# A hybrid FoX/GLA decoder layer: gate folded into W_o, residual rows summed half-way, and FFN operands made in the order of their products

## The chip, the core and the metric

One core of one Trainium2 chip. The metric is the device time of one execution in microseconds (us), given as the median of several runs. Engines: TensorE (PE; its weight loads PEld), VectorE (DVE), ScalarE (ACT), GpSimd (POOL), and SyncE (SP), which issues the transfers.

## What is computed

One decoder layer of 1024 rows and width 1024, in float32. The parts that matter here, from the reference:

```python
u = x * (1.0 + scale_m) + shift_m
proj = u @ w_in                                  # FoX and GLA columns
...
y = jnp.concatenate([fox_out, gla_out], axis=-1) @ w_o
x = layer_norm(DEEPNORM_ALPHA * x + (1.0 + gate_m) * y, ln1_g, ln1_b)
u2 = x * (1.0 + scale_f) + shift_f
h = jax.nn.silu(u2 @ w_gate) * (u2 @ w_up)       # 1024 -> 2816
y2 = h @ w_down
x = layer_norm(DEEPNORM_ALPHA * x + (1.0 + gate_f) * y2, ln2_g, ln2_b)
```

## The kernel before

**Arithmetic.** Every float32 operand of a large product is split into a high part (a rounding cast by ACT, L87) and a low part (a subtraction by VectorE, L88). A product is three matmuls: high by high, high by low, low by high. `split` and `load_split` do this; a W_o load passes through a "raw" buffer (a ring of three, shared with other loads) and is split into buffers "hi" and "lo".

**Order.** A scheduler with a timeline simulation sets the order of the instructions on each engine; within an engine they run in that order. `tc.issue_after` (and `after(key)`) keeps what it encloses behind a named instruction.

**Stages.** Input projection and GLA come first (to about 366 us of the span). The FoX stage follows (366 to 572 us), in 16 steps of scores, softmax and values; into its first 12 steps 16 *fills* are put, `woproj_gla(h, t)`: 12 matmuls (L664 to L666) of the GLA half of y for a tile of 128 rows and 512 columns, an ACT copy to a raw buffer, and a store to the scratch tensor `yp_d`. The mixer's end runs in two halves of 512 rows, each of 8 *units* (`mixer_units`, 4 row tiles by 2 column halves h): 12 matmuls of the FoX half of y in a PSUM bank "yo" (L845 to L847), then VectorE adds the stored part (L848), POOL multiplies by the gate row `gm` (L849), VectorE forms alpha x + y (L850) and the LayerNorm statistics (L789); after h = 1 the row is scaled by ACT (L857) and stored. `mixer_loads` brings the rows of x and of `yp_d`, `mixer_weights` the FoX rows of W_o. The first half's units lie in the last FoX steps, the second half's behind them, up to 607 us.

**FFN.** Rows of u2 are transposed (u2p, L873) and scaled by ACT (L874), the first half of rows into tiles `af`, the second into `x2` (for the fourth chunk a raw buffer); a *chunk* j is 128 of the first 512 features together with 128 of the second 512. Gate and up products of one group f of 128 hidden columns (22 groups) are made by a Strassen-like form, with seven products of 12 matmuls (L965): p1 = B11 A11 and p2 = B21 A12 into "gu"; T3 S3 and T4 A22 into "gx"; T1 S1 and B22 S4 into "gy"; T2 S2 into "gz". A are quarters of u2 (A22 of the second rows), S1 to S4 their sums (S1 = A21 + A22, S3 = A11 - A21, S2 = S1 - A11, S4 = A12 - S2); B and T are quarters of the weights and their sums. `first_operands` makes A11 and A12; `second_operands` makes A22 and, chunk by chunk, S1 with S3 and then S2 with S4 (L910 to L919); `first_weights` splits the gate weights, `sum_weights` makes B22 and T1 to T4 (L947 on, sums L951 to L954). Five products (p1 of groups 0, 1, 2, p2 of 0 and 1) are queued behind the last unit, ahead of all products that use S. Later groups need no new S.

Of the kernel before, what the change touches and what calls it, by code (L numbers as in the profile page):

```python
# [33 lines left out]
def hymba_layer_kernel(  # L34
# [399 lines left out]
    wa2 = mp.tile([P, 256], F32R, tag="m1", name="wa2")[0:80]  # L434
# [73 lines left out]
    def gla_pair(p, n):  # L508
# [20 lines left out]
        osb = mp.tile([P, 256], F32, tag="m1", name=nm("osb"))  # L529
# [116 lines left out]
    yp_d = dp.tile([S, D], F32, name="yp_d")  # L646
    wo_g = {}

    def woproj_gla(h, t):
# [10 lines left out]
        ts = slice(t * P, (t + 1) * P)  # L660
        ps = bank("b3", "yg")
        for k in range(4):
            wh, wl = wo_g[h][k // 2]
            nc.tensor.matmul(ps, ogh[k][:, ts], wh[:, k % 2, :], start=k == 0, stop=False)  # L664
            nc.tensor.matmul(ps, ogh[k][:, ts], wl[:, k % 2, :], start=False, stop=False)
            nc.tensor.matmul(ps, ogl[k][:, ts], wh[:, k % 2, :], start=False, stop=k == 3)  # L666
# [137 lines left out]
    YS = ((4, 5, 6, 7), (10, 11, 12, 13))  # L804

    def mixer_loads(half):
        rt, yt = [], []
        for q in range(4):
            t = 4 * half + q
            r = slot(XS[half][q], name="r")  # L810
            nc.sync.dma_start(r, xr[t * P : (t + 1) * P, :])
            rt.append(r)
            y = slot(YS[half][q], name="yp")
            nc.sync.dma_start(y, yp_d[t * P : (t + 1) * P, :])
            yt.append(y)
        return rt, yt

    def mixer_weights(h):
        return [
            load_split(  # L820
                (2, 512),
                w_o[g * 256 : (g + 1) * 256, h * 512 : (h + 1) * 512].rearrange("(k p) n -> p k n", p=P),
            )
            for g in range(2)
        ]
# [4 lines left out]
    def mixer_units(half, rt, yt):  # L830
# [36 lines left out]
    S_HL = ((0, 1, 2, 3, 10), (11, 12, 13, 26, 27), (28, 29, 30, 31, 36), (20, 21, 22, 23, 37))  # L867
# [24 lines left out]
    def second_operands(rt):  # L892
# [7 lines left out]
        ops = {n: [] for n in ("A22", "S1", "S2", "S3", "S4")}  # L900
# [4 lines left out]
        for j in range(NJ):  # L905

            t = slot(S_HL[j][4], (2, 512), dt=F32R, name="a22")
            split(t[:, 0, :], t[:, 1, :], xs[j][:, 1, :])
            ops["A22"].append((t[:, 0, :], t[:, 1, :]))
            nc.vector.tensor_tensor(xs[j][:, 1, :], xs[j][:, 0, :], xs[j][:, 1, :], op=ALU.add)  # L910
            nc.vector.tensor_tensor(xs[j][:, 0, :], af[j][:, 0, :], xs[j][:, 0, :], op=ALU.subtract)
            hi = slot(S_HL[j][0], (2, 512), dt=F32R, name="s31h")
            lo = slot(S_HL[j][1], (2, 512), dt=F32R, name="s31l")
            split(hi, lo, xs[j])
            ops["S3"].append((hi[:, 0, :], lo[:, 0, :]))
            ops["S1"].append((hi[:, 1, :], lo[:, 1, :]))
        for j in range(NJ):
            nc.vector.tensor_tensor(af[j][:, 0, :], xs[j][:, 1, :], af[j][:, 0, :], op=ALU.subtract)
            nc.vector.tensor_tensor(af[j][:, 1, :], af[j][:, 1, :], af[j][:, 0, :], op=ALU.subtract)  # L919
            hi = slot(S_HL[j][2], (2, 512), dt=F32R, name="s24h")  # L920
            lo = slot(S_HL[j][3], (2, 512), dt=F32R, name="s24l")
            split(hi, lo, af[j])
            ops["S2"].append((hi[:, 0, :], lo[:, 0, :]))
            ops["S4"].append((hi[:, 1, :], lo[:, 1, :]))
        opnd.update(ops)
# [46 lines left out]
    def group_parts(f, w):  # L972
# [157 lines left out]
    for idx, (hp, i) in enumerate(steps):  # L1130
# [9 lines left out]
        if idx < len(nfill):  # L1140
            for _ in range(nfill[idx]):
                with (tc.issue_after(lastsc[(2, 2)].ins) if idx == 11 else nullcontext()):
                    woproj_gla(*fills.pop(0))
        if hp == 3 and i == 0:
            gm = wtile("raw", (D,), F32)
            nc.sync.dma_start(gm, grow_d[0, :].partition_broadcast(P))
            xa, ya = mixer_loads(0)
            late = mixer_units(0, xa, ya)
# [5 lines left out]
    xb, yb = mixer_loads(1)  # L1154
# [4 lines left out]
    for f in mixer_units(1, xb, yb):  # L1159
        f(3)  # L1160
    first_weights(load_gate(2), ws[2])
    second_operands(xb)
    gs = [group_parts(f, ws[f]) for f in range(3)]
    with after("yo"):
# [4 lines left out]
        gs[2][0]()  # L1169
    for f in range(NF):  # L1170
        if f < 3:
            p1, p2, p754, p63 = gs[f]
            w = ws[f]
            g = load_gate(f)
# [50 lines left out]
```

## Time and profile before

| | |
|---|---|
| median of the runs | 1318.05 us (1318.05, 1318.34, 1313.09) |
| the profiled execution | 1315.98 us, span 1314.2 us |
| busy, of the span | PE 96%, DVE 58%, ACT 38%, POOL 19% |
| mean granted TensorE clock | 0.989 of full |
| FoX stage, 366 to 572 us | PE 204.99 of 206 us busy |
| 560 to 660 us, in 20 us windows | PE 18.15, 17.57, 18.86, 6.57, 19.56 |

Times of the trace are us from the span's start. A row names the source line, the engine, the operation, out<-in by the program's names, and the shape; "xN" is a count. The median is over whole executions, and the trace is one of them.

### The profile page before, as it was taken

Reading aid. Unit: us, or ns where it says so; the run is one execution under the profiler, and the core shown is the slowest. Engines: PE = TensorE matmul, PEld = TensorE weight load, DVE = VectorE, ACT = ScalarE, POOL = GpSimd, SP = SyncE. Lnnn points to the kernel's source line nnn. Section 1 sums busy time; section 2 is a strip of 40 time slices with the busy share of each in tenths; the row PEclk is TensorE's granted clock in tenths of the full one; section 3 lists DMA queues with packets and bytes.
Section 4 is the critical chain, followed back from the end, with each engine's and each line's share of the span. In section 5 each row is a group of like instructions: output and inputs, shape, how many; then the busy total and the mean of one; then the engine's idle time right before and its main releaser. Section 6 shows DMA issues by size and latency. Waiting matters only on the chain.

```text
span 1314.2 us, 16370 instructions
## 1 busy us (share of the span) xinstructions
PE 1259.9 (96%) x6341; PEld 1018.3 (77%) x6341; DVE 756.2 (58%) x1093; ACT 497.1 (38%) x834; POOL 244.6 (19%) x244
## 2 busy tenths in 40 slices
PE   5999999999999999998599999999999999999997
PEld 4888987899876766667488888888888878788885
DVE  7665547732345546567965565565565576484346
ACT  3423355523265566464532233233323322411331
POOL 3500123320033435433000000000000076010004
PEclk9999999999999999999799999999999999999999
DMA  9875611102013206542342322321331474644431
GB/s 299 256 228 177 207 50 33 33 9 65 1 49 98 56 27 226 176 152 97 99 142 80 96 78 68 96 92 53 97 97 48 142 279 152 203 153 129 129 128 64
DMA packets 123534, 153.17 MB, mean 117 GB/s; under 512 B 6480, under 2 KB 86458, under 8 KB 123456
## 3 DMA queue, kind: packets, MB, share of 16 engines
q1 hardware_dynamic: 123456, 152.12, 36.1%
q8 instruction: 50, 0.82, 0.3%
q14 instruction: 28, 0.23, 0.1%
HBM read 123.64 MB, written 24.13 MB: 112 GB/s over the span
## 4 chain that ended last, share of the span: by engine, by line
PE 77%; DMA 8%; DVE 7%; ACT 3%; issue 2%; POOL 1%; SPq 1%; POOLq 0%; DVEq 0%; ACTq 0%
PE gx L965 9%; PE gy L965 9%; PE gu L965 9%; DMA wc<-in_w_c_dram 5%; PE dn L1059 5%; PE dn L1061 5%; PE dn L1060 5%; PE gz L965 5%; PE pv L756 4%; PE tr L746 3%; PE acc L330 2%; PE acc L331 2%; PE acc L332 2%; PE acc L100 2%; PE acc L101 2%
## 5 line engine op out<-in xcount | busy, mean ns | idle before, releaser
L88 DVE TENSOR_TENSOR lo<-raw,hi 128x1024 fp32r<-128x1024 f32 (+1 forms) x108 | 146.3, 1356 | 258.6 <-ACT hi L87 258.5
L87 ACT CAST hi<-raw 128x1024 fp32r<-128x1024 f32 (+1 forms) x108 | 113.1, 1049 | 192.3 <-PE dn L1061 79.3
L330 PE MATMUL acc<-hi,uh 128*128 128x264 f32 (+1 forms) x384 | 108.1, 282 | 1.0 <-ACT osb L530 0.8
L331 PE MATMUL acc<-lo,uh 128*128 128x264 f32 (+1 forms) x384 | 108.2, 282 | 0.0
L332 PE MATMUL acc<-hi,ul 128*128 128x264 f32 (+1 forms) x384 | 108.1, 282 | 0.0
L1032 POOL TENSOR_TENSOR r<-r,l1g 128x1024 f32<-128x1024 f32 x8 | 24.3, 3068 | 436.3 <-DMA r<-z_d 436.3
L1060 PE MATMUL dn<-lo,hh 128*128 128x512 f32 x256 | 101.2, 395 | 0.0
L1061 PE MATMUL dn<-hi,hl 128*128 128x512 f32 x256 | 100.8, 395 | 0.0
L1059 PE MATMUL dn<-hi,hh 128*128 128x512 f32 x256 | 94.2, 396 | 4.1 <-ACT hi L87 2.1
L721 DVE CUSTOM_DVE_ANT_0 pr<-sc,smask 128x128 f32<-128x128 f32 (+7 forms) x64 | 47.9, 755 | 55.2 <-PE sc L717 31.5
L330 PEld LDWEIGHTS acc<-hi,uh 128*128 128x128 f32 x384 | 72.2, 188 | 2.1 <-ACT osb L530 1.0
L331 PEld LDWEIGHTS acc<-lo,uh 128*128 128x128 f32 x384 | 72.2, 188 | 0.7 <-issue 0.5
L332 PEld LDWEIGHTS acc<-hi,ul 128*128 128x128 f32 x384 | 72.1, 188 | 0.3 <-issue 0.2
L965 PE MATMUL gu<-a1h,hi 128*128 128x512 f32 x160 | 63.6, 397 | 0.0
L965 PE MATMUL gu<-a1l,hi 128*128 128x512 f32 x160 | 63.5, 397 | 0.0
L965 PE MATMUL gu<-a1h,lo 128*128 128x512 f32 x160 | 63.3, 396 | 0.0
L731 POOL TENSOR_SCALAR pr<-pr,sm 128x128 f32<-128x128 f32 (+7 forms) x64 | 52.1, 816 | 57.3 <-DVE sm L728 56.8
L751 ACT COPY pt<-tr 128x512 f32<-128x512 f32 x80 | 46.1, 582 | 43.9 <-PE tr L746 42.3
L756 PE MATMUL pv<-pt,fv 128*64 128x256 f32 x320 | 61.4, 396 | 0.5 <-DVE ofl L88 0.5
L1059 PEld LDWEIGHTS dn<-hi,hh 128*128 128x128 f32 x256 | 48.2, 189 | 16.6 <-ACT hi L87 2.8
L100 PE MATMUL acc<-ul,hi 128*128 128x512 f32 x144 | 58.0, 403 | 0.0
L101 PE MATMUL acc<-uh,lo 128*128 128x512 f32 x144 | 57.9, 402 | 0.0
(305 smaller groups left out, 3103.0 us busy)
## 6 DMA issues: line engine op xcount, KB each, us to landing
raw<-in_w_down_dram SPq DMA_DIRECT2D x44, 512.0 KB, 3.9
wc<-in_w_c_dram SPq DMA_DIRECT2D x32, 512.0 KB, 4.4
raw<-in_w_gate_dram SPq DMA_DIRECT2D x25, 512.0 KB, 3.9
h_d<-hf SPq DMA_DIRECT2D x22, 512.0 KB, 2.7
hr<-h_d SPq DMA_DIRECT2D x22, 512.0 KB, 3.9
u<-in_w_up_dram SPq DMA_DIRECT2D x21, 512.0 KB, 3.8
wc<-in_w_c_dram SPq DMA_DIRECT2D x32, 256.0 KB, 6.7
raw<-in_w_in_dram SPq DMA_DIRECT2D x15, 512.0 KB, 4.0
```

The source lines that it names most:

```text
L87: nc.scalar.copy(dst_hi, src)
L88: nc.vector.tensor_tensor(dst_lo, src, dst_hi.bitcast(F32), op=ALU.subtract)
L100: nc.tensor.matmul(ps, lh, rl, start=False, stop=False)
L101: nc.tensor.matmul(ps, ll, rh, start=False, stop=stop)
L330: nc.tensor.matmul(ps, uh[k][:, ts], wh[:, k % 4, :], start=k == 0, stop=False)
L331: nc.tensor.matmul(ps, uh[k][:, ts], wl[:, k % 4, :], start=False, stop=False)
L332: nc.tensor.matmul(ps, ul[k][:, ts], wh[:, k % 4, :], start=False, stop=k == NK - 1)
L756: nc.tensor.matmul(pv[64 * par : 64 * par + 64, 0:256], fv_t(kb)[:, 64 * h : 64 * h + 64], pt[:, par, a * 256 : (a + 1) * 256], start=kb == 0,
L965: nc.tensor.matmul(ps, x, y, start=start and j == 0 and i == 0, stop=j == NJ - 1 and i == 2, skip_group_check=not start,)
L1059: nc.tensor.matmul(ps, hh, wh, start=i == 0 and a == 0, stop=False)
L1060: nc.tensor.matmul(ps, hh, wl, start=False, stop=False)
L1061: nc.tensor.matmul(ps, hl, wh, start=False, stop=i == NF // 2 - 1 and a == 1)
```

## The change

1. **Gate in W_o.** `wo_load` loads 256 rows by 512 columns of W_o, and POOL multiplies both blocks by `gm` (two 128x512 operations per load, 24 in all) ahead of the split. The units' 16 multiplies go. `gm` takes one raw buffer from the first FoX step to the last W_o load.
2. **Half-way rows.** A fill ends with one VectorE operation, alpha x + PSUM, on an x tile of 128x512 loaded for it (three tiles in turn), stored to `rp_d`; 16 x loads are added, the ACT copies go. `mixer_loads` reads four tiles of `rp_d` per half where it read four of x and four of `yp_d`. A unit is one add (PSUM + r), then the statistics.
3. **Operands in the order of the products.** `second_operands` is made in stages, all four chunks of one operand before the next: S3, S1, A22, S2, S4, each in 128x512 pieces.
4. **Group 0's weight sums** (`sum_weights(0)`) stand after the fifth of the second half's eight units; they stood behind `second_operands`.
5. **Six products** are queued ahead of the S products: p2 of group 2 is added; its p1 is copied to a tile of its own.
6. Storage: osb, wa2, B22 and one S3 tile take other slots.

```diff
     def split(dst_hi, dst_lo, src):
         nc.scalar.copy(dst_hi, src)
-        nc.vector.tensor_tensor(dst_lo, src, dst_hi.bitcast(F32), op=ALU.subtract)
+        return nc.vector.tensor_tensor(dst_lo, src, dst_hi.bitcast(F32), op=ALU.subtract).ins
...
+    def wo_load(r0, h, slots=None):
+        raw = wtile("raw", (2, 512), F32)
+        hs = slice(h * 512, (h + 1) * 512)
+        nc.sync.dma_start(raw, w_o[r0 : r0 + 256, hs].rearrange("(k p) n -> p k n", p=P))
+        for k in range(2):
+            nc.gpsimd.tensor_tensor(raw[:, k, :], raw[:, k, :], gm[:, hs], op=ALU.mult)
...
+        split(hi, lo, raw)
+        return hi, lo
...
+    def x_load(n):
+        if n < 2 * NT:
+            h, t = divmod(n, NT)
+            b = xbuf[:, n % 3, :] if n % 3 < 2 else xlast
+            nc.sync.dma_start(b, xr[t * P : (t + 1) * P, h * 512 : (h + 1) * 512])
+            xt.append(b)
...
-        yt = wtile("raw", (512,), F32)
-        nc.scalar.copy(yt, ps)
-        nc.sync.dma_start(yp_d[ts, h * 512 : (h + 1) * 512], yt)
+        with after("yg"):
+            x_store()
+        b = xt[n]
+        nc.vector.scalar_tensor_tensor(b, b, ALPHA, ps, op0=ALU.mult, op1=ALU.add)
+        yt.append((h, t, b))
+        with tc.issue_after(ins.ins):
+            x_load(n + 2)
...
-            nc.vector.tensor_tensor(yp[:, hs], ps, yp[:, hs], op=ALU.add)
-            nc.gpsimd.tensor_tensor(yp[:, hs], yp[:, hs], gm[:, hs], op=ALU.mult)
-            nc.vector.scalar_tensor_tensor(r[:, hs], r[:, hs], ALPHA, yp[:, hs], op0=ALU.mult, op1=ALU.add)
+            nc.vector.tensor_tensor(r[:, hs], r[:, hs], ps, op=ALU.add)
...
+        stage("S3", 0, a11, a11, a21, ALU.subtract, "t")
+        stage("S1", 1, a21, a21, a22, ALU.add, "sS3")
+        stage("A22", 4, a22, None, None, None, "sS1")
+        stage("S2", 2, a22, a22, a11, ALU.subtract, "lo")
+        stage("S4", 3, a12, a12, a22, ALU.subtract, "sS2")
...
-    for f in mixer_units(1, xb, yb):
+    late = mixer_units(1, xb)
+    for f in late[:5]:
+        f(3)
+    g = load_gate(0)
+    sum_weights(0, g, load_up(0), ws[0])
+    for f in late[5:]:
         f(3)
     first_weights(load_gate(2), ws[2])
-    second_operands(xb)
+    x2 = second_rows(xb)
+    second_operands(x2)
...
         gs[2][0]()
+        gs[2][1]()
```

A stage makes, for each chunk, one sum (VectorE) and its split (ACT cast, VectorE subtraction); its last argument names the instruction behind which it is issued ("t" the last split of group 0's T, "lo" the last split of A22, "sS3" the last S3 difference, and so on). Line numbers in the rows of the changed order are those of the changed file.

**Places in the order.** TensorE, at the end of the last product that needs no S (names: b1 and hi/lo of a gu row are gate weights of a group, a1 operands A11 and A12; hi_1005 and hi_921 hold T3 and T2 of group 0, hi_1007 and hi_923 T1 and T4). Before:

```order
L965 MATMUL gu_998_5740<-a1h_922_5397,b1_934_5427 128x512
L965 MATMUL gu_998_5740<-a1h_927_5414,b1_933_5426 128x512
L965 MATMUL gu_998_5740<-a1l_928_5415,b1_933_5426 128x512
L965 MATMUL gu_998_5740<-a1h_927_5414,b1_934_5427 128x512
L965 MATMUL gx_1009_5825<-s31h_979_5685,hi_1005_5817 128x512
L965 MATMUL gx_1009_5825<-s31l_980_5686,hi_1005_5817 128x512
L965 MATMUL gz_1011_5865<-s24h_990_5718,hi_1005_5817 128x512
L965 MATMUL gz_1011_5865<-s24l_991_5719,hi_1005_5817 128x512
L965 MATMUL gy_1010_5839<-s31h_979_5685,hi_1007_5821 128x512
```

Now:

```order
L996 MATMUL gu_966_5738<-a1h_888_5385,b1_894_5397 128x512
L996 MATMUL gu_966_5738<-a1l_889_5386,b1_894_5397 128x512
L996 MATMUL gu_966_5738<-a1h_888_5385,b1_895_5398 128x512
L996 MATMUL gx_970_5818<-s3_946_5663,hi_921_5530 128x512 x2
L996 MATMUL gx_970_5818<-s3_946_5663,lo_922_5531 128x512
L996 MATMUL gx_970_5818<-s3_947_5667,hi_921_5530 128x512 x2
L996 MATMUL gx_970_5818<-s3_947_5667,lo_922_5531 128x512
L996 MATMUL gx_970_5818<-s3_948_5671,hi_921_5530 128x512
```

Before, gx, gz and gy took turns by single matmuls as chunk 0's operands came; now whole chunks of S3 follow one another, and the first gy stands behind two of them and a half. Ahead of the first gx stand now, from the first gu on, 36 gu matmuls, 16 transposes, 22 gu matmuls, 16 transposes and 14 gu matmuls; the first matmul with the low part of group 1's T3 and T2 is the 135th that is no transpose.

VectorE behind the last LayerNorm row (af are the first rows, x2 and raw_937/raw_969 the second; L88 the low parts; L951 and L952 sums of group 0's weights). Before:

```order
L88 TENSOR_TENSOR a22_978_5680<-x2_966_5628,a22_978_5680 128x512
L910 TENSOR_TENSOR x2_966_5628<-x2_966_5628 128x512
L911 TENSOR_TENSOR x2_966_5628<-af_909_5350,x2_966_5628 128x512
L88 TENSOR_TENSOR a22_981_5689<-x2_967_5629,a22_981_5689 128x512
L918 TENSOR_TENSOR af_909_5350<-x2_966_5628,af_909_5350 128x512
L910 TENSOR_TENSOR x2_967_5629<-x2_967_5629 128x512
L919 TENSOR_TENSOR af_909_5350<-af_909_5350 128x512
L951 TENSOR_TENSOR raw_1002_5806<-raw_1003_5808,raw_1002_5806 128x512
L911 TENSOR_TENSOR x2_967_5629<-af_914_5367,x2_967_5629 128x512
L88 TENSOR_TENSOR s31l_980_5686<-x2_966_5628,s31h_979_5685 128x1024
L88 TENSOR_TENSOR a22_984_5698<-x2_968_5630,a22_984_5698 128x512
```

Now (L943 is a stage's sum):

```order
L943 TENSOR_TENSOR af_870_5321<-af_870_5321,x2_934_5610 128x512
L943 TENSOR_TENSOR af_875_5338<-af_875_5338,x2_935_5611 128x512
L88 TENSOR_TENSOR s3_946_5663<-af_870_5321,s3_946_5663 128x512
L88 TENSOR_TENSOR s3_947_5667<-af_875_5338,s3_947_5667 128x512
L943 TENSOR_TENSOR af_880_5355<-af_880_5355,x2_936_5612 128x512
L943 TENSOR_TENSOR af_885_5372<-af_885_5372,raw_937_5613 128x512
L943 TENSOR_TENSOR x2_934_5610<-x2_934_5610 128x512
L943 TENSOR_TENSOR x2_935_5611<-x2_935_5611 128x512
L943 TENSOR_TENSOR x2_936_5612<-x2_936_5612 128x512
L943 TENSOR_TENSOR raw_937_5613<-raw_937_5613 128x512
L88 TENSOR_TENSOR a22_954_5694<-x2_934_5610,a22_954_5694 128x512
L88 TENSOR_TENSOR a22_955_5697<-x2_935_5611,a22_955_5697 128x512
```

Before, A22, S1, S3, S2 and weight sums alternate chunk by chunk; now the four S3 differences and four S1 sums come first, and group 0's weight sums are no longer there. From the first S1 sum (x2_934) to the low part of group 1's T3 and T2, that one included, VectorE has 40 operations: 39 of 128x512 and one of 128x1024; sums of the weights of groups 1 and 2 and two of gz's and gy's sums are among them.

POOL, at the second half's units (mv is the LayerNorm scale). Before, the multiplies of the units (raw_806 is the gate row):

```order
L796 TENSOR_TENSOR mv_896_5279<-mv_896_5279,half_neg_81 128x1
L796 TENSOR_TENSOR mv_898_5303<-mv_898_5303,half_neg_81 128x1
L796 TENSOR_TENSOR mv_900_5327<-mv_900_5327,half_neg_81 128x1
L849 TENSOR_TENSOR yp_902_5336<-yp_902_5336,raw_806_4850 128x512
L849 TENSOR_TENSOR yp_904_5340<-yp_904_5340,raw_806_4850 128x512
L849 TENSOR_TENSOR yp_906_5344<-yp_906_5344,raw_806_4850 128x512
L849 TENSOR_TENSOR yp_908_5348<-yp_908_5348,raw_806_4850 128x512
```

Now, the multiplies of the W_o loads (raw_421 is the gate row), of the second half's column halves 0 and 1:

```order
L661 TENSOR_TENSOR raw_900_5405<-raw_900_5405,raw_421_3013 128x512 x2
L831 TENSOR_TENSOR mv_861_5262<-mv_861_5262,half_neg_81 128x1
L831 TENSOR_TENSOR mv_863_5284<-mv_863_5284,half_neg_81 128x1
L831 TENSOR_TENSOR mv_865_5306<-mv_865_5306,half_neg_81 128x1
L661 TENSOR_TENSOR raw_903_5413<-raw_903_5413,raw_421_3013 128x512 x2
L661 TENSOR_TENSOR raw_910_5481<-raw_910_5481,raw_421_3013 128x512 x2
L661 TENSOR_TENSOR raw_913_5489<-raw_913_5489,raw_421_3013 128x512 x2
L831 TENSOR_TENSOR mv_917_5512<-mv_917_5512,half_neg_81 128x1
```

The multiplies stood behind each unit's matmuls, and now stand ahead of the splits that the matmuls use.

## Rows read from the trace of the kernel before

**Rows 1.** The page, part 1: engine, busy us, share of the span, instructions.

```profile
PE 1259.9 (96%) x6341; PEld 1018.3 (77%) x6341; DVE 756.2 (58%) x1093; ACT 497.1 (38%) x834; POOL 244.6 (19%) x244
```

**Rows 2.** Waits of TensorE, 560 to 660 us: us in total, times, longest.

```profile
PE gx L965 <- ACT hi L87: 13.1, 1, 13.1
PE yo L845 <- ACT hi L87: 2.0, 2, 1.3
PE yo L846 <- DVE lo L88: 1.8, 1, 1.8
PE yo L845 <- DVE yp L848: 1.5, 1, 1.5
```

**Rows 3.** Windows (us: busy of PE, PEld, DVE, ACT, POOL; granted clock; DMA share, GB/s).

```profile
580.00:600.00 20.00, 17.57 (x84) 13.50 (x84) 18.23 (x18) 12.74 (x16) 7.29 (x4) 1.00 0.35 123
...
700.00:1060.00 360.00, 360.00 (x1556) 293.23 (x1555) 209.67 (x258) 111.84 (x148) 9.25 (x4) 1.00 0.29 93
```

**Rows 4.** Windows cut at the first gu, the first gx and the clock's return.

```profile
606.79:637.60 30.81, 17.71 (x94) 14.43 (x92) 22.79 (x42) 21.35 (x28) 5.14 (x6) 0.86 0.44 136
637.60:646.27 8.67, 7.90 (x17) 5.46 (x18) 8.67 (x11) 5.24 (x6) 0.00 (x0) 0.50 0.41 97
```

**Rows 5.** Timeline of TensorE, 606 to 650 us: start, us, instruction [idle before].

```profile
606.79 0.40 PE L965 MATMUL gu<-a1h,b 128*128 128x512 f32 x1
...
619.60 1.91 PE L873 MATMUL u2p<-ident,r 128*128 128x128 f32 x16
...
624.11 0.39 PE L965 MATMUL gu<-a1h,b 128*128 128x512 f32 x1
637.60 0.79 PE L965 MATMUL gx<-s31h,hi 128*128 128x512 f32 x1 [13.10 <-ACT hi L87]
...
646.30 0.40 PE L965 MATMUL gx<-s31h,hi 128*128 128x512 f32 x1
...
649.54 0.40 PE L965 MATMUL gz<-s24l,hi 128*128 128x512 f32 x1
```

**Rows 6.** Timeline of VectorE, 620 to 628 us.

```profile
626.01 0.68 DVE L911 TENSOR_TENSOR x<-af,x 128x512 f32<-128x512 f32 x1
626.61 1.22 DVE L88 TENSOR_TENSOR s31l<-x,s31h 128x1024 fp32r<-128x1024 f32 x1
627.75 0.68 DVE L88 TENSOR_TENSOR a<-x,a 128x512 fp32r<-128x512 f32 x1
```

**Rows 7.** Timeline of ScalarE (ACT), 617 to 637 us.

```profile
617.61 2.78 ACT L874 ACTIVATE x<-u2p,mcol 128x512 f32<-128x512 f32 x4 [1.64 <-PE u2p L873]
...
636.50 1.04 ACT L87 CAST hi<-raw 128x1024 fp32r<-128x1024 f32 x1
```

**Rows 8.** Timeline of GpSimd (POOL), 583 to 592 us: the gate multiplies.

```profile
583.82 4.38 POOL L849 TENSOR_TENSOR yp<-yp,raw 128x512 f32<-128x512 f32 x2 [11.52 <-DVE yp L848]
591.81 1.30 POOL L849 TENSOR_TENSOR yp<-yp,raw 128x512 f32<-128x512 f32 x1 [3.61 <-DVE yp L848]
```

**Rows 9.** DMA issues: queue, count, size of each, median us to landing.

```profile
raw<-in_w_o_dram SPq DMA_DIRECT2D x12, 512.0 KB, 4.3
...
stk<-stk SPq DMA_DIRECT2D x16, 256.0 KB, 3.2
yp_d<-raw SPq DMA_DIRECT2D x16, 256.0 KB, 2.0
```

**Rows 10.** Windows in the FoX stage.

```profile
520.00:560.00 40.00, 40.00 (x208) 27.90 (x207) 24.82 (x48) 20.42 (x39) 17.31 (x18) 1.00 0.46 158
```

**Rows 11.** Two short gaps of TensorE in its timeline.

```profile
215.04 0.33 PE L533 MATMUL kt<-ident,gk 128*128 128x128 f32 x1 [2.50 <-POOL gk L500]
...
1143.50 1.20 PE L1059 MATMUL dn<-hi,hh 128*128 128x512 f32 x4 [2.08 <-ACT hi L87]
```

**Rows 12.** Windows behind these two gaps.

```profile
215.00:220.00 5.00, 4.96 (x15) 3.94 (x16) 5.00 (x7) 1.51 (x3) 0.62 (x1) 0.66 0.01 2
...
1145.00:1150.00 5.00, 5.00 (x17) 3.99 (x16) 3.10 (x3) 2.00 (x2) 0.00 (x0) 0.70 0.79 254
```

More of the change, by code (lines that the diff above doesn't have):

```diff
@@ L432, in log_sigmoid @@
         nc.vector.tensor_tensor(t0[0:n], t0[0:n], t1[0:n], op=ALU.add)
-    wa2 = mp.tile([P, 256], F32R, tag="m1", name="wa2")[0:80]
+    wa2 = slot(36, (256,), dt=F32R, name="wa2")[0:80]
+    m1 = cp.tile([P, 512], F32, tag="m1", name="m1")
     nc.gpsimd.memset(wa2.bitcast(F32), 0.0)
@@ L528, in gla_pair @@
             nc.tensor.matmul(o[:, h * P : (h + 1) * P], am[n % 2][h], vs, start=(n == 0), stop=(n == 0 or h == 1))
-        osb = mp.tile([P, 256], F32, tag="m1", name=nm("osb"))
+        osb = m1[:, p * 256 : (p + 1) * 256]
         nc.scalar.copy(osb, o[:, 0:256])
@@ L663, in woproj_gla @@
             wh, wl = wo_g[h][k // 2]
[L664 removed]
+            ins = nc.tensor.matmul(ps, ogh[k][:, ts], wh[:, k % 2, :], start=k == 0, stop=False)
+            if k == 0:
+                last["yg"] = ins.ins
             nc.tensor.matmul(ps, ogh[k][:, ts], wl[:, k % 2, :], start=False, stop=False)
[L666 to L669 removed]
+            ins = nc.tensor.matmul(ps, ogl[k][:, ts], wh[:, k % 2, :], start=False, stop=k == 3)
+        with after("yg"):
[5 more added lines that the diff above has]
+            x_load(n + 2)
     stk = {}
@@ L810, in mixer_loads, with mixer_weights @@
             r = slot(XS[half][q], name="r")
-            nc.sync.dma_start(r, xr[t * P : (t + 1) * P, :])
+            nc.sync.dma_start(r, rp_d[t * P : (t + 1) * P, :])
             rt.append(r)
[L813 to L818, printed above, removed]
-        return [
[L820 to L824, printed above, removed]
+        return rt
+    def mixer_weights(half, h):
+        return [
+            wo_load(g * 256, h, (10 + 2 * g, 11 + 2 * g) if (half, h) == (1, 1) else None) for g in range(2)
         ]
@@ L828, in hymba_layer_kernel, with mixer_units @@
     ybank = [0]
-    def mixer_units(half, rt, yt):
+    def mixer_units(half, rt):
         bs = [new_bs() for q in range(4)]
@@ L890, in first_operands, with put, second_rows @@
             opnd[name] = [(h[:, a, :], l[:, a, :]) for h, l in ops]
-    def second_operands(rt):
+    def put(ops, name, i, src):
+        t = slot(i, (2, 512), dt=F32R, name=name.lower())
+        last["lo"] = split(t[:, 0, :], t[:, 1, :], src)
+        ops[name].append((t[:, 0, :], t[:, 1, :]))
+    def second_rows(rt):
         xs = []
@@ L903, in second_operands, with stage @@
                 u2_rows(rt, j + NJ * a, xs[j][:, a, :], ("b0", "b1", "b2", "b3")[2 * (j % 2) + a])
[L905 to L924, printed above, removed]
+        return xs
+    def second_operands(xs):
+        ops = {n: [] for n in ("A22", "S1", "S2", "S3", "S4")}
+        def stage(name, i, out, x, y, op, key):
+            with after(key):
+                for j in range(NJ):
+                    if op is None:
+                        ins = None
+                    else:
+                        ins = nc.vector.tensor_tensor(out(j), x(j), y(j), op=op)
+                        last["s" + name] = ins.ins
+                    put(ops, name, S_HL[j][i], out(j))
+        a11, a12 = (lambda j: af[j][:, 0, :]), (lambda j: af[j][:, 1, :])
+        a21, a22 = (lambda j: xs[j][:, 0, :]), (lambda j: xs[j][:, 1, :])
+        stage("S3", 0, a11, a11, a21, ALU.subtract, "t")
[3 more added lines that the diff above has]
+        stage("S4", 3, a12, a12, a22, ALU.subtract, "sS2")
         opnd.update(ops)
@@ L956, in sum_weights @@
             h, l = wtile("hi", (NK, P), F32R), wtile("lo", (NK, P), F32R)
-            split(h, l, raw)
+            last["t"] = split(h, l, raw)
             w[n0], w[n1] = (h[:, 0:NJ], l[:, 0:NJ]), (h[:, NJ:NK], l[:, NJ:NK])
@@ L983, in p2 @@
         def p2():
-            h = st_["h"] = slot(6 + par, (2, 512), name="hf")
-            nc.scalar.copy(h[:, 0, :], c11)
+            if f == 2:
+                st_["p1"] = cp.tile([P, 512], F32, tag="m1", name="p1c")
+            else:
+                st_["h"] = slot(6 + par, (2, 512), name="hf")
+                st_["p1"] = st_["h"][:, 0, :]
+            nc.scalar.copy(st_["p1"], c11)
             product(c11, w["B21"], opnd["A12"], False)
         def p754():
+            if f == 2:
+                st_["h"] = slot(6 + par, (2, 512), name="hf")
             h = st_["h"]
@@ L1143, in hymba_layer_kernel @@
                     woproj_gla(*fills.pop(0))
+        if not fills:
+            x_store()
         if hp == 3 and i == 0:
[L1145 to L1148, printed above, removed]
+            xa = mixer_loads(0)
+            late = mixer_units(0, xa)
         fox_values(hp, i, cur)
@@ L1173, in hymba_layer_kernel @@
             w = ws[f]
[L1174 removed]
+            if f > 0:
+                g = load_gate(f)
         else:
```

50 lines of the change are left out of this document (29 added, 21 removed).

## The prediction

> **What bounds the kernel now.** I read the page first: TensorE is busy 96% of the span [rows 1], so time can only be won where it stands still or runs slowly. The waits of TensorE between 560 and 660 us come next [rows 2]: one wait of 13.1 us, of the first gx matmul for an ACT cast, and four short ones of the mixer's second half, 2.0 + 1.8 + 1.5 = 5.3 us together. Then the windows: from 700 to 1060 us TensorE is busy throughout at full clock [rows 3], so the FFN after its start gives nothing.
>
> The stretch around the long wait is read from the windows cut at its ends [rows 4]. From 606.79 (first gu matmul) to 637.60 (first gx matmul) TensorE worked 17.71 of 30.81 us. From 637.60 to 646.27 it ran at granted clock 0.50, the 1.2 GHz level, after having stood idle for 13.1 us. The timeline gives the price of a matmul there: fourteen steps from 646.30 to 649.54, 0.231 us each; the 16 transposes of 619.60 take 1.91 us [rows 5]. Work done from 606.79 to 646.27: 60 gu matmuls and 17 later ones, 77 × 0.231 = 17.8, and 32 transposes, 3.8; together 21.6 of 39.5 us. **The start of the FFN loses 17.9 us**, wait and slow clock together.
>
> Why the wait is so long stands in VectorE's timeline [rows 6]: it works without a pause, an operation of 128x512 every 0.60 us and a split of 128x1024 every 1.14, and takes operands of all four sums, and weight sums, in the order in which they fall due by the schedule, not in which TensorE wants them. The cast that ends the wait, of group 0's weight sum T, starts at 636.50 [rows 7], because its sums are behind operands that no matmul wants yet.
>
> **The change, part by part.**
>
> *Group 0's weight sums among the last units.* The 4 VectorE sums (0.60 each), 2 splits (1.14) and a 0.60 split of B22 leave the queue after the last unit: about 5.3 us less there, and T is ready before gx wants it. The same 5.3 us now lie beside 8 units of 12 matmuls, 22 us; VectorE was busy 18.23 of 20 us from 580 on [rows 3], so the room must come from the next item.
>
> *No gate multiply and no alpha pass in a unit.* A unit loses one VectorE pass (16 × 0.60 = 9.6 us over both halves, 4.8 in the second) and 16 POOL multiplies. Its chain after the last matmul loses about 0.6 + 1.3 us, so the bank comes free sooner and the last LayerNorm row is done sooner; the wait of 1.5 us for a bank's evacuation, and 1.8 us for a split queued behind such passes, go [rows 2]. What is added: each W_o load gets two POOL multiplies of 1.30 [rows 8] between its transfer (4.3 us [rows 9]) and its cast, 2.6 us later in a chain in which the raw buffers are used again one after the other; and the gate row holds one of three raw buffers throughout. This lengthens the two ACT-cast waits, unless the loads are issued sooner. I take the removed waits at 5.3, and 0.6 for what comes back at a bank: **4.8 us**, the first gu matmul at 602.0. Ends: 1 us (the multiplies take the place of the casts' waits) and 6.
>
> *Alpha x + y stored half-way.* In the FoX stage ACT's 16 copies become 16 VectorE operations on PSUM, with 16 x loads of 256 KB beside the 16 stores; the mixer reads one tile per row in place of two. TensorE is busy 40.00 of 40 us from 520 to 560 [rows 10] and VectorE 24.82, so there is room on VectorE and no wait to win. I take 0, ends −1.5 and +1.5 from a wait of a few tenths at some of the fills; the cover is that a fill's bank is not wanted at once.
>
> *Operands in the order of the products; six products queued.* Total work is unchanged; what counts is when the last operand of each product is ready. With the first gu matmul at 602.0: 36 matmuls (8.3) and 16 transposes (1.9) to 612.2, 22 matmuls (5.1) and 16 transposes to 619.2, 14 matmuls (3.2) to 622.4, when gx wants S3 of chunk 0. ACT evacuates at 0.70 each, four in 2.78 us [rows 7]: chunks 2 and 3 are complete at 619.2 and 620.6. VectorE then takes the fourth S3 difference at 620.6 and from 621.2 on 39 operations of 0.60 and one split of 1.14 up to the low part of group 1's T, 24.5 us: done at **645.7**. TensorE meets that operand as its 135th FFN matmul; without any wait it would be there at 602.0 + 135 × 0.231 + 3.8 = 637.0. So the operands are late by about 9 us, spread: S3 of chunk 2 is split at 626.0 where TensorE wants it at 624.3 (1.7), then 0.5 at chunk 3, 1.8, 0.9, 1.1 and 0.9 at the S2 chunks, and 1.8 at group 1's T. From there VectorE is ahead. **Loss 9.0 in place of 17.9**, if no wait lasts long enough to cost clock. What clock it costs: gaps of 2.50 and 2.08 us elsewhere were followed by stretches at about half clock (the 5 us windows behind them show 0.66 and 0.70 [rows 11, 12]), while the waits of 1.8 and 1.5 us in the mixer's second half [rows 2] were not: the clock was 1.00 from 580 to 600 [rows 3]. All my waits are at or under 1.8, but close together; half a slow stretch, 1.5 us, is charged. Ends: 0 and 7 (a slow stretch as long as the one before). The sixth product itself costs nothing and pays 12 × 0.231 = 2.8 us of cover.
>
> *The rest* (osb's tile, wa2's slot, slots 3 and 24, the copy of p1) moves storage only: 0.
>
> **Sum.** 1315.98 − 4.8 (second half) − (17.9 − 9.0 − 1.5 = 7.4) ± 0 = 1303.8 against the profiled execution, which lies 2.1 us below the median of the runs shown (1318.05). Carried to that median it is 1305.9; since one of the three runs was at 1313.09, I take 1305.5. About 0.5%, 6.6 us, is what a measurement of this kernel can tell from no change: faster is below 1311.5, slower above 1324.6.
>
> **The rivals.**
>
> *B: the clock falls in the string of waits.* By my sum TensorE is idle some 9 us between 624 and 646, in seven pieces. If the granted clock goes to the 1.2 GHz level there, matmuls are 0.43 apart and not 0.231; some 60 of them cost 11.7 us more, of which the waits for operands absorb about 7. Result: 5 us more, 1309 to 1311. For it: two gaps hardly over 2 us were enough [rows 11, 12]. Against: shorter single gaps were not. The Trainium skill (TensorE: Matmul & The Clock Gate, section "A second HAM failure mode: psum-queue depth-cycling") says that a TensorE which idles briefly and often between groups of matmuls can swing between its two clocks; by that rule B would be the likeliest case, and no stretch of this trace shows such a string. Chance 0.13.
>
> *C: the POOL multiplies run beside VectorE at twice the time.* Of the 16 multiplies of before, two next to each other took 4.38 us and one 1.30 [rows 8]. At 2.2 each, a W_o load's chain is 4.4 us longer and not 2.6; two loads in series give 3.6 us more, and with the one held buffer the whole 4.8 of the second half is lost: 1310. The Trainium skill (SBUF — State Buffer, section "SBUF: two separate sides") says that VectorE and GpSimd share a pair of ports which one instruction locks while the other blocks; the two rows agree with it as far as they go. Chance 0.10.
>
> *E: the wait moves whole.* VectorE's queue stays the bound, and another operand (S2, S4 or the sums of groups 1 and 2, which are put between them) is late by as much as T was: of the 7.4 us nothing comes. 1311 to 1317. For it: VectorE was busy 8.67 of 8.67 us in the slow stretch [rows 4], and loses only 5.3. Against: 72 matmuls and then 24 more stand before S1's users. Chance 0.09.
>
> *D: slower, by the FoX stage.* VectorE now carries x + y of each fill in order, between the softmax passes, and each waits for its x tile. The load into a tile waits for the store of its last user: store 2.0 and load 3.2 (the same size from the stack copies) [rows 9], 5.2 us in one queue with everything else that SP issues. A tile's turn is three fills of 12 matmuls each, 8.3 us at the least, so it is covered. It decides if SP's queue holds a load back by over 3 us where fills are dense, for then VectorE stands at a fill, and the softmax passes behind it, and TensorE after them: 16 fills × 1.5 us = 24 us, minus the 12.2 won: 1316 + 24 − 12 = 1328, 1330 by the median. The gate's multiplies of the first W_o loads, placed ahead of probability scalings on POOL, work the same way. Chance 0.06.
>
> **The numbers.** Forecast 0.62 with 1301 to 1309 as its own range; B 0.13, C 0.10, E 0.09, D 0.06. Faster: 0.60 of the forecast, 0.10 of B, 0.06 of C, 0.01 of E: 0.77. Slower: 0.06. The same: 0.17. The range goes from 1298 (the second half's 6, no clock lost, and a run low by a few us, as one of the three was) to 1313, which takes in B and C and a part of E.
>
> **What would show it.** Right: no TensorE wait above 2.5 us between 600 and 660; a string of waits for low parts (VectorE) of S3, S2 and one T; first gu matmul at 601 to 604; granted clock above 0.9 in 620 to 650; TensorE at 40.00 of 40 in the FoX stage. Wrong: one wait above 5 us at gx, gy or gz (E); clock near 0.5 after 620 with only short waits (B); W_o multiplies at over 2 us and first gu matmul after 605 (C); waits of pv, tr or yg in 370 to 570 that grew to several us (D).

## Result and profile after

The changed kernel takes **1305.46 us** in the median (1304.18 to 1307.24, 5 runs), the kernel before, timed beside it, 1317.27 (1313.09 to 1318.34). The ratio is 0.992, with a 95% interval of 0.9898 to 0.9941: 11.8 us faster, where 1305.5 was forecast. The time came out as predicted; the split behind it did not. The profiled execution took 1304.18 us, span 1302.4, against 1315.98 and 1314.2.

The page, part 1, of the changed kernel, answering to [rows 1]; TensorE's work is the same and its share of the span hardly moves:

```profile
PE 1256.3 (96%) x6341; PEld 1017.0 (78%) x6341; DVE 756.9 (58%) x1101; ACT 489.2 (38%) x826; POOL 259.6 (20%) x252
```

Its waits of TensorE from 560 to 660 us (total, times, longest), answering to [rows 2]. The 13.1 us are gone, and nothing above 1.4 us has come in their place; but the units ("yo") still wait 3.3 us, now for VectorE's add:

```profile
PE yo L872 <- DVE r L875: 3.3, 3, 1.3
PE gz L996 <- DVE s L88: 2.6, 3, 0.9
PE gx L996 <- DVE s L88: 1.6, 2, 1.4
PE gz L996 <- DVE lo L88: 0.6, 1, 0.6
PE u2p L898 <- ACT af L899: 0.5, 1, 0.5
```

The timeline of TensorE, answering to [rows 5]: first gu, first gx, the longest wait, and the 135th FFN matmul, which waits for the low part of group 1's T:

```profile
606.63 0.39 PE L996 MATMUL gu<-a1h,b 128*128 128x512 f32 x1
...
626.68 0.62 PE L996 MATMUL gx<-s,hi 128*128 128x512 f32 x2
...
630.07 0.50 PE L996 MATMUL gx<-s,hi 128*128 128x512 f32 x1 [1.39 <-DVE s L88]
...
649.86 0.50 PE L996 MATMUL gz<-s,lo 128*128 128x512 f32 x1 [0.56 <-DVE lo L88]
```

The first gu matmul stands at 606.63, not at the 602.0 of the forecast, 0.16 us from where it was. I cut each profiled execution at three marks of TensorE's timeline: the first fill (yg), the first gu matmul, and the start of the 300th FFN matmul from there (gu, gx, gy and gz; transposes left out). The columns are us of those stretches; "rest" is what lies behind.

| kernel | to first fill | FoX and mixer | FFN's first 300 | rest | span | median of its runs |
|---|---|---|---|---|---|---|
| before | 363.0 | 243.8 | 90.8 | 616.6 | 1314.2 | 1317.27 |
| changed | 361.6 | 245.0 | 81.5 | 614.3 | 1302.4 | 1305.46 |
| e1 sums back | 362.2 | 241.8 | 93.6 | 613.6 | 1311.1 | 1315.41 |
| e2 old order | 362.8 | 244.7 | 83.2 | 616.8 | 1307.5 | 1308.76 |
| e3 line of p2 out | 365.1 | 244.6 | 81.5 | 614.5 | 1305.7 | 1304.51 |
| e4 mixer's parts | 363.6 | 242.4 | 86.7 | 613.6 | 1306.3 | 1308.04 |
| f1 FFN's parts | 363.6 | 243.2 | 94.1 | 615.0 | 1315.8 | 1317.26 |
| f2 gate alone | 364.0 | 245.2 | 89.4 | 615.7 | 1314.2 | 1316.83 |
| f3 sums on POOL | 364.0 | 245.2 | 87.3 | 615.5 | 1311.8 | 1312.23 |
| f4 three banks | 364.0 | 242.7 | 84.6 | 616.2 | 1307.5 | 1308.38 |
| g1 five, no tile | 361.7 | 244.3 | 84.3 | 614.6 | 1304.9 | 1309.6 |
| g2 mixer, no tile | 365.4 | 242.2 | 90.1 | 615.2 | 1312.9 | 1313.35 |
| g3 up early | 364.7 | 243.3 | 81.5 | 613.7 | 1303.1 | 1305.28 |
| h1 sums behind | 361.4 | 242.3 | 79.9 | 613.9 | 1297.4 | 1301.54 |

Timed beside the experiments below, the kernel before had a median of 1316.1 to 1316.7; their ratios are to that. The first column spreads over 4 us and the fourth over 3.2, so I argue from the two in between, and from medians. In these two columns the change lost 1.2 us up to the first gu and won 9.3 behind it; the other 3.7 of the 11.8 lie in the outer columns.

### The profile page after: what moved, and what is told of

Its sections match the earlier page's. It is cut to its first block, busy times and chain, and to the rows that moved or that the text cites. A ratio compares the mean times of both kernels' runs of the same rounds, so it can differ in the third digit from the quotient of the medians.

```text
span 1302.4 us, 16377 instructions
## 1 busy us (share of the span) xinstructions
PE 1256.3 (96%) x6341; PEld 1017.0 (78%) x6341; DVE 756.9 (58%) x1101; ACT 489.2 (38%) x826; POOL 259.6 (20%) x252
## 4 chain that ended last, share of the span: by engine, by line
PE 75%; DMA 9%; DVE 7%; ACT 3%; issue 2%; POOL 2%; SPq 0%; POOLq 0%; DVEq 0%; ACTq 0%
PE gu L996 9%; PE gx L996 9%; PE gy L996 9%; DMA wc<-in_w_c_dram 5%; PE dn L1096 5%; PE dn L1098 5%; PE dn L1097 5%; PE gz L996 4%; PE pv L791 4%; PE tr L781 3%; PE acc L330 2%; PE acc L332 2%; PE acc L331 2%; PE acc L100 2%; DMA raw<-in_w_down_dram 2%
## 5 line engine op out<-in xcount | busy, mean ns | idle before, releaser
L88 DVE TENSOR_TENSOR lo<-raw,hi 128x1024 fp32r<-128x1024 f32 (+1 forms) x106 | 144.3, 1363 | 243.7 <-ACT hi L87 243.6
L87 ACT CAST hi<-raw 128x1024 fp32r<-128x1024 f32 (+1 forms) x106 | 110.8, 1048 | 204.8 <-PE dn L1098 83.2
L996 PE MATMUL gy<-s,b 128*128 128x512 f32 x264 | 64.8, 393 | 0.2 <-ACT s L87 0.2
L760 ACT ACTIVATE pr<-pr,sm 128x128 f32<-128x128 f32 (+7 forms) x64 | 49.8, 778 | 33.4 <-DVE sm L756 31.6
L996 PE MATMUL gz<-s,hi 128*128 128x512 f32 x176 | 59.5, 399 | 2.6 <-DVE s L88 2.6
```

The source lines that it names most:

```text
L88: return nc.vector.tensor_tensor(dst_lo, src, dst_hi.bitcast(F32), op=ALU.subtract).ins
L760: nc.scalar.activation(t[:, 0:nk], t[:, 0:nk], AF.Exp, bias=sm[:, 0:1], scale=-1.0, accum_out=sm[:, 1:2])
L996: nc.tensor.matmul(ps, x, y, start=start and j == 0 and i == 0, stop=j == NJ - 1 and i == 2, skip_group_check=not start,)
```

## Experiments

**One part undone at a time.** e1: `sum_weights(0)` returns behind `second_operands`.

```diff
-    late = mixer_units(1, xb)
-    for f in late[:5]:
-        f(3)
-    g = load_gate(0)
-    sum_weights(0, g, load_up(0), ws[0])
-    for f in late[5:]:
+    for f in mixer_units(1, xb):
         f(3)
...
-            if f > 0:
-                g = load_gate(f)
+            g = load_gate(f)
...
-        if f > 0:
-            sum_weights(f, g, load_up(f), w)
+        sum_weights(f, g, load_up(f), w)
```

> The changed kernel with group 0's weight sums moved back behind the second rows' operands. Theory 1 (VectorE's queue at the FFN's start sets the time): its 5.3 us of sums and splits stand in that queue again, first gu matmul as in the changed kernel (606 to 607 us) or 0.5 earlier, one wait of 5 to 13 us for T in place of the short ones, 1310 to 1316 us. Rival 1 (the sixth product and the order of the stages carry the gain, T only has to come after them): 1305 to 1307 us.

1315.41 us, ratio to before 0.9995 (0.9985 to 1.0005): all of the gain is gone. The waits of TensorE show where: the whole chain of S operands now stands ahead of T.

```profile
PE gx L996 <- ACT hi L87: 15.3, 1, 15.3
```

So theory 1 holds for this part. But "FoX and mixer" fell to 241.8: without the sums among the units that stretch is 3.2 us shorter than in the changed kernel.

e2: the operands chunk by chunk (`second_operands` as before), the rest as changed.

> The changed kernel with the second rows' operands made chunk by chunk as before (A22, S1 and S3 of each chunk, then S2 and S4), group 0's weight sums left among the units, six products queued. Theory 1: less of VectorE's work is wanted first; the 4 A22 and 4 S1 pieces stand ahead of the last S3, waits of 3 to 6 us more, 1308 to 1312 us. Rival 1 (only T was late; the order of the stages moves waits about): 1304 to 1307 us.

1308.76 (0.9942; 0.993 to 0.9955): 3.3 us of the 11.8, at the low end of theory 1. One wait for S3's cast, 3.9 us, takes the place of the short ones; the first 300 lose 1.7, "rest" 2.5.

e3: the line `gs[2][1]()` taken out, p2 of group 2 in the loop again.

> The changed kernel with five products queued and not six. Theory 1: VectorE's chain to the low part of group 1's T ends at the same time, and TensorE has 2.8 us less to do until then, so 1307 to 1309 us, unless the order puts that product into a wait further on. Rival 1 (TensorE's supply is not what counts): 1304.5 to 1306.5 us.

1304.51, the same as the changed kernel. It tested nothing: 72 matmuls stand ahead of gx with the line and without it, since the scheduler put the product there by itself. What lets it is the tile of its own for p1, so g1 takes that away too, and there 60 stand ahead.

e4: only the gate fold and the half-way rows (with the storage of the change).

> Only the gate fold and the half-way rows: the changed kernel with group 0's sums, the order of the operands and the five products as before. Theory 1: the mixer's parts give nothing, the FoX stage pays what the second half wins, the first gu matmul stands at 606 to 608 us and the start of the FFN loses 16 to 19 us: 1314 to 1318 us. Rival 2 (the mixer's parts are worth the 4.8 us of the forecast, and the changed trace shows them late by chance): 1310 to 1313 us.

1308.04 (0.994; 0.9928 to 0.9953). **Both theories miss: the mixer's parts and the storage alone give 8.4 us**, and not where I had put it: 1.4 in "FoX and mixer", 4.1 in the FFN's first 300. 72 matmuls stand ahead of gx here too, so the tile's sixth product is in it.

**The halves alone.** f1: the FFN's parts without the mixer's.

> Only the FFN's parts: the kernel before with the order of the operands, group 0's sums among the last units and six products as in the change; gate, half-way rows and units as before (the second half's last W_o columns go to slots of their own, as in the change). Theory 3 (from the four runs so far: the mixer's shorter chain behind the last unit is what starts the operands sooner, the FFN's parts add little by themselves): the units get 3 to 5 us longer, since VectorE and POOL already had their own work there, the FFN's start loses 9 to 12 us in place of 17.9, together 1311 to 1316 us. Rival (theory 1 as forecast: the FFN's parts carry most of the gain): 1305 to 1309 us.

1317.26 (1.0007; 0.9998 to 1.0015): nothing, and above both ranges. The timeline of ACT in f1 shows the last rows scaled at 616.87 to 624.46, 10 to 18 us behind its first gu matmul at 606.81; its waits show TensorE standing for group 2's weights already in the first products:

```profile
616.87 2.37 ACT L862 ACTIVATE r<-r,mv 128x1024 f32<-128x1024 f32 x2
619.39 1.24 ACT L862 ACTIVATE r<-r,mv 128x1024 f32<-128x1024 f32 x1 [0.15 <-DVE mv L859]
623.21 1.25 ACT L862 ACTIVATE r<-r,mv 128x1024 f32<-128x1024 f32 x1
```

```profile
PE gu L976 <- ACT hi L87: 4.1, 1, 4.1
```

VectorE is busy 36.39 of 40 us from 580 to 620 there, so it has little room for group 0's sums while the units keep their two passes. The forecast had named this condition and then charged nothing for it. VectorE is not shown to be the only cause: the sums' first operation, at 602.73, waited for the load of the up weights, and the load of group 2's weights was issued at 611.64, behind the first gu. The two were not parted.

f2: the gate in W_o, all else as before.

> Only the gate folded into W_o: each unit keeps the VectorE passes of before (add of the stored part, alpha x + y) and the loads of x and of the stored part. Theory 3: the POOL multiply of 1.3 us leaves each unit's chain, the last LayerNorm row is done 1.5 to 3 us sooner after the first gu matmul than the 9.2 us of before, and half or more of what the mixer's parts gave (8.4 us) is there: 1310 to 1314 us. Rival (the half-way rows carry it, since VectorE is the bound and the gate was on POOL): 1315 to 1318 us. If the multiplies ahead of the W_o splits hold TensorE (rival C of the prediction): over 1318 us.

1316.83 (1.0002; 0.9993 to 1.001): nothing, so the rival holds. The multiplies ahead of the W_o splits do not make it slower either. What pays in the mixer is the gate and the half-way rows together, or the rows alone; rows without the gate in W_o can't be stored half-way in this form, and were not tried.

**The sixth product.** g1 is e3 without the tile for p1 (p1 is copied to `h` of the group, as before); g2 is e4 without it.

```diff
-            if f == 2:
-                st_["p1"] = cp.tile([P, 512], F32, tag="m1", name="p1c")
...
+            h = st_["h"] = slot(6 + par, (2, 512), name="hf")
+            nc.scalar.copy(h[:, 0, :], c11)
```

> The changed kernel with five products queued and without the tile of its own for group 2's p1, so that the sixth product cannot come ahead of gx (with the tile, the order put it there anyway when only the line was taken out). Theory 1: VectorE's chain to the low part of group 1's T ends when it did, TensorE has 2.8 us less to do until then and does them later: 1307.5 to 1309 us, the first 300 FFN matmuls 2 to 3 us longer than in the changed kernel. Rival (the product takes up no wait, since the waits are short and spread): 1304.5 to 1306.5 us.

> Only the gate fold and the half-way rows, as in e4_mixer_only, and now without the tile of its own for group 2's p1, so that five products stand ahead of gx as before. Theory 3: what of the 8.4 us was the sixth product (2.8 us) goes, the shorter chain of the units stays: 1310 to 1312 us, first gx matmul after a wait of 10 to 12 us. Rival (the mixer's parts carry all of it): 1307.5 to 1309 us. If the mixer's parts alone are worth nothing and the tile carried it: 1314 to 1318 us.

g1: 1309.6 (0.995; 0.9937 to 0.9963), the first 300 2.8 us longer than in the changed kernel. g2: 1313.35 (0.9972; 0.9961 to 0.9983), the first 300 3.4 longer than in e4. Both medians lie above the range of theory 1 or 3, g1 by 0.6 and g2 by 1.4. The product fills about the 2.8 us that its 12 matmuls take; the medians moved by more, 4.1 and 5.3, and where the difference of 1 to 2 us lies is open. So the mixer's parts by themselves are worth 3.4 us, and the product about 3 to 5.

**What still bounds it.** f3: weight sums of groups 1 and 2 by `nc.gpsimd` in place of `nc.vector`.

> The changed kernel with the weight sums of groups 1 and 2 (8 operations of 128x512) on POOL, which does nothing from 614 us on. If VectorE's chain to the low part of group 1's T is the bound: its 6 sums in that chain, 3.6 us, go, POOL has 1.3 us for each and time enough, the FFN's start loses 5 in place of 8.3 us, 1301.5 to 1303.5 us. Rival (POOL and VectorE lengthen each other, as in the two gate multiplies of 2.2 us each): VectorE's pitch rises over 0.60 beside them, or POOL's operations take over 2 us, 1304.5 to 1308 us.

1312.23 (0.9963; 0.9951 to 0.9976), 6.8 us worse than the changed kernel. The rival's direction, by far more than its size. The timeline of POOL in f3, and its longest wait of TensorE:

```profile
633.39 11.68 POOL L983 TENSOR_TENSOR raw<-u,raw 128x512 f32<-128x512 f32 x1 [19.98 <-issue]
645.14 1.59 POOL L984 TENSOR_TENSOR u<-u 128x512 f32<-128x512 f32 x1
646.70 1.25 POOL L983 TENSOR_TENSOR raw<-u,raw 128x512 f32<-128x512 f32 x1
```

```profile
PE gz L997 <- ACT hi L87: 9.2, 1, 9.2
```

One subtraction of POOL, 1.25 us elsewhere, took 11.68: from 633.61 to 645.6 VectorE ran 19 operations back to back. The first 17 have both inputs in SBUF and kept their usual 0.60 us; the 18th has one input in PSUM (gy), and POOL's operation ended 1.23 us behind its start; the 19th, with both in SBUF again, took 1.18 us where the others show 0.69 or 0.70. VectorE's timeline, the last two:

```profile
643.84 0.70 DVE L1033 TENSOR_TENSOR hf<-gy,hf 128x512 f32<-128x512 f32 x1
644.44 1.18 DVE L88 TENSOR_TENSOR s<-af,s 128x512 fp32r<-128x512 f32 x1
```

By these times POOL got its turn at VectorE's first operation with fewer than two inputs in SBUF, while VectorE went on. The changed kernel has the same pattern in small: a W_o multiply of POOL, started at 587.77 beside a split of VectorE, ended 1.24 us behind the start of LayerNorm statistics (588.82, one input), and the split behind those, at 589.43, took 1.71 us in place of 1.23. The Trainium skill (SBUF — State Buffer, "SBUF: two separate sides") says that the pair of ports the two share is locked for a whole instruction and that the other blocks fully; these rows agree, with 11.68 against 1.25 us for POOL and 1.18 against 0.69 for VectorE's 19th operation.

f4: three PSUM banks for the second half's units.

> The changed kernel with three PSUM banks in turn and not two for the second half's units. If a unit of the changed kernel waits for its bank because VectorE's add stands behind group 0's sums: the three waits of 1.35, 0.88 and 1.07 us go, the first gu matmul is 2 to 3.3 us sooner. What remains of it at the end depends on the last row's LayerNorm, which VectorE sets: theory 1, 1302 to 1303.5 us; rival (the FFN's start is timed by VectorE, so TensorE only waits later): 1304.5 to 1306.5 us.

1308.38 (0.9935; 0.9923 to 0.9946), 2.9 worse than the changed kernel and above both ranges. "FoX and mixer" won 2.3 us as expected, the first 300 lost 3.1, "rest" 1.9. TensorE ran ahead, but the last rows are scaled when VectorE is done with them (it ends their scales from 612.69 to 614.08), 6.2 us and more behind the first gu (606.65):

```profile
612.87 4.64 ACT L882 ACTIVATE r<-r,mv 128x1024 f32<-128x1024 f32 x4
```

g3: group 0's up weights loaded into a slot, so that the load need not wait for a raw buffer.

> The changed kernel with group 0's up weights loaded into slot 7 and not into a raw buffer, so that their load does not wait for the last W_o loads to leave the ring. If the units and the last LayerNorm row are late because group 0's sums start late (VectorE stood 1.86 us for that load at 595.59) and then stand among the last units' adds: sums 2 us sooner, the last row scaled 1 to 2 us sooner, 1302.5 to 1304.5 us. Rival (VectorE's work in the units is the bound, whenever it starts): 1305 to 1306.5 us.

1305.28 (0.9918; 0.9905 to 0.9931): the median did not move, as the rival had it. The trace is nearer to the theory: the units' waits for VectorE's add are 1.5 us in place of 3.3, and "FoX and mixer" is 243.3 in place of 245.0. That execution took 3.1 us more ahead of the first fill, where the edit changes nothing. Whether the 1.7 us are real is open.

**A better version.** The sums are far too early where the change put them, while VectorE stands still behind them. The timeline of VectorE in the changed kernel: T's second split at 603.97, where gx and gy want T from 626.68 on; and 6.15 us idle ahead of the first S3 difference.

```profile
603.97 1.17 DVE L88 TENSOR_TENSOR lo<-raw,hi 128x1024 fp32r<-128x1024 f32 x1
...
617.31 0.69 DVE L943 TENSOR_TENSOR af<-af,x 128x512 f32<-128x512 f32 x1 [6.15 <-ACT x L899]
```

h1 puts them into that gap ("mv" is the instruction that ends a row's LayerNorm scale, of the last row here):

```diff
-    for f in late[:5]:
-        f(3)
-    g = load_gate(0)
-    sum_weights(0, g, load_up(0), ws[0])
-    for f in late[5:]:
+    for f in late:
         f(3)
     first_weights(load_gate(2), ws[2])
+    g = load_gate(0)
+    u = load_up(0)
+    with after("mv"):
+        sum_weights(0, g, u, ws[0])
```

> The changed kernel with group 0's weight sums behind the last row's LayerNorm statistics, ahead of the second rows' operands, where VectorE stood still for 6.15 us in the changed kernel (until 617.31). If those 5.3 us of sums among the units' adds are what made the units wait and the last rows late: the waits of the units fall from 3.3 us to about 1.2, the stretch from the first fill to the first gu matmul goes from 245.0 to about 242.3 us, the last row is scaled some 4 us after the first gu matmul and not 7, and the FFN's first 300 matmuls stay at 80.5 us: 1302 to 1303.5 us. Rival (VectorE's work at the FFN's start is the bound, and the sums there push every operand back by what the units win): the first 300 matmuls take 82.5 to 84 us, 1304.5 to 1307 us.

**1301.54 us** (1299.14 to 1305.68, 6 runs), ratio 0.9901 (0.9884 to 0.9918); the forecast side, a little below its range. "FoX and mixer" is 242.3, the number expected; the first 300 are 79.9 (the 80.5 of the expectation is the 81.5 of the table). The last row is scaled 3.0 to 4.3 us behind the first gu matmul (603.68), where it was 2.3 to 7.0 for the four in the changed kernel and 7.9 to 9.2 for the last in the one before. ACT's timeline, of the kernel before, the changed one and h1:

```profile
614.73 1.24 ACT L857 ACTIVATE r<-r,mv 128x1024 f32<-128x1024 f32 x1 [0.21 <-DVE mv L854]
```

```profile
608.96 4.64 ACT L882 ACTIVATE r<-r,mv 128x1024 f32<-128x1024 f32 x4 [5.32 <-DVE mv L879]
```

```profile
606.72 1.25 ACT L882 ACTIVATE r<-r,mv 128x1024 f32<-128x1024 f32 x1 [1.33 <-DVE mv L879]
```

The waits of TensorE in h1 from 560 to 660 us: the units' 3.3 are 1.1.

```profile
PE gx L996 <- ACT hf L1029: 1.4, 1, 1.4
PE gz L996 <- DVE lo L88: 1.1, 1, 1.1
PE yo L872 <- DVE r L875: 1.1, 1, 1.1
```

Against the changed kernel this is 3.9 us by the medians and 4.3 in the two columns (2.7 + 1.6); the two intervals against the kernel before overlap, and the two were not timed side by side.

## Why the prediction was right, and where it was not

**What bounds the kernel**: right. The 9.3 us won in the FFN's first 300 matmuls are the wait at gx and the slow clock behind it.

**Operands in the order of the products**: right in its mechanism and in the length of VectorE's work, counted from the first gu matmul; the waits came out shorter. Forecast: the low part of group 1's T done 43.7 us behind it; measured 43.2 (649.81). Waits forecast 1.7 and 0.5 at S3's chunks 2 and 3, 1.8, 0.9, 1.1 and 0.9 at S2's chunks, 1.8 at T; measured 1.39 and 0.23, then none, 0.95, 0.83 and 0.84, and 0.56. Of the 7.4 us forecast this became 9.3. The term that was forecast too large is the loss that stays: 9.0 + 1.5 at the 135th matmul, against 8.2 measured there (649.86 − 606.63 us, less the 135 × 0.231 + 3.8 of work), of which clock is a part.

**The clock** (rival B): it did fall, late and briefly, as charged and not as the rival had it. The windows of the changed kernel, answering to [rows 4]:

```profile
620.00:640.00 20.00, 17.25 (x79) 12.64 (x77) 17.58 (x29) 13.20 (x24) 0.00 (x0) 1.00 0.22 59
640.00:660.00 20.00, 17.53 (x67) 13.05 (x67) 19.93 (x29) 10.19 (x14) 0.00 (x0) 0.91 0.48 148
```

A mean of 0.91 over 20 us, behind three waits of 0.8 to 0.95; in h1, with waits of 0.84, 0.93 and 1.12 us, the clock is 1.00 throughout. The Trainium skill (TensorE: Matmul & The Clock Gate, "A second HAM failure mode: psum-queue depth-cycling") has the clock swing with such a string of idle moments; the changed kernel agrees to that extent, at 1.8 us (9% of 20) and not the 5 of the rival, and h1, with its full clock, does not.

**The second half, 4.8 us**: wrong. The step that failed is that of group 0's weight sums among the last units ("so the room must come from the next item"), charged at nothing. With the sums among them the stretch up to the first gu matmul takes 245.0 us, with the sums behind (h1) or back (e1) 242.3 and 241.8: the sums cost 2.7 to 3.2. Without them the mixer's parts win 1.5 there, not 4.8, since the FoX stage, part of that stretch, gives back some (next item). The units' waits themselves were sized about right: 5.3 us before [rows 2], 3.3 with the sums among the units, 1.1 in h1.

**The FoX stage, 0 ± 1.5**: outside its bounds on its own. TensorE was busy 204.99 of 206 us from 366 to 572, and now:

```profile
366.00:572.00 206.00, 202.55 (x1103) 140.49 (x1101) 113.73 (x270) 111.01 (x234) 86.76 (x116) 1.00 0.31 95
```

Waits that were not there before, from its timeline:

```profile
462.31 0.35 PE L751 MATMUL sc<-stk,stk 128*128 128x256 f32 x1 [0.70 <-DMA stk<-stk]
...
466.45 0.39 PE L751 MATMUL sc<-stk,stk 128*128 128x256 f32 x1 [0.86 <-DVE sm L756]
...
502.11 0.50 PE L872 MATMUL yo<-hi,ofh 128*128 128x512 f32 x1 [1.00 <-DVE xbuf L701]
```

By what ended them, these look like rival D's mechanisms in small: more transfers in SP's queue, and a fill's sum behind other work of VectorE while its bank is wanted; no run tested them. They are 2.6 us and not 24.

**Rival C**: not so. POOL's multiplies took 1.29 us in the median of 24; four took over 1.5, the longest 2.34:

```profile
L661 POOL TENSOR_TENSOR raw<-raw,raw x24: 1267/1294/2342, 322.6 to 587.8; 128x512 f32<-128x512 f32 x24
```

**Rival E**: not so with the change whole, but e1 is it: T wanted first and made last gives back everything.

**The sixth product**: right, 2.8 and 3.4 us for the 2.8. **The sum**: right by chance. 6 us too much in the second half (4.8 won was forecast, 1.2 lost was measured) were made up by 1.9 more at the FFN's start and 3.7 in stretches to which I had given nothing: 1.4 ahead of the FoX stage, where the clock fell in the execution before and not in the changed one (last section), and 2.3 in "rest", where the last group's waits of 0.94 and 1.11 us at the first W_down products (at 1064.0 and 1066.9 us before) are gone. Why they are gone was not tested.

**The parts are not additive.** The FFN's parts alone give 0, the mixer's parts with the tile 8.4, both 11.8. I had added terms as if each stood alone; by f1's rows, the mixer's relief of VectorE is what the FFN's sums were paid from.

## What to carry to other kernels

Where one engine's in-order queue feeds the bound engine, ask of each item in it when it is wanted: sums made 20 us too early hold up the work in front of which they stand (2.7 us here; the same sums too late cost all of the gain), and the place for them is the queue's own idle gap (here worth 3.9 us more than the change). Cost a moved step at the place where it goes, not only at the one it leaves, and test parts together as well as apart. An idle engine is not free room if it shares a path with the busy one.

## What was not expected of the hardware

A POOL operation on two SBUF tiles stood for 11.68 us beside an unbroken run of 17 VectorE operations on two SBUF tiles, which kept their 0.60 us. It did not wait for a pause: it ended 1.23 us behind the start of the 18th, which has an input in PSUM, and then the 19th was the one that stood (1.18 us). Elsewhere a POOL operation of this shape took 1.25 to 2.3.

The same gap of TensorE can cost clock or not. The gap of 2.50 to 2.51 us at 215 us is in all 14 profiled executions; the granted clock behind it was below 1 in 9 of them (0.66 in the one before [rows 12]) and full in 5. The window of the changed kernel:

```profile
215.00:220.00 5.00, 4.82 (x21) 3.94 (x22) 5.00 (x7) 1.90 (x4) 0.76 (x2) 1.00 0.00 2
```

This alone moves an execution by about 1.4 us (the last kt transpose at 259.79 us before, at 258.37 in the changed kernel).
